# Two thirds of a layer's modulation weights read in another stage, and one third's columns written by themselves

## The chip, the core and the metric

The kernel runs on one core of a Trainium2 chip. A core has a matrix engine (TensorE, PE in the rows; PEld is its weight load), a vector engine (VectorE, DVE), an activation engine (ScalarE, ACT), a general engine (GpSimd, POOL) and SyncE (SP), which here only issues transfers. Each engine works through its own instructions in order and waits on semaphores for the others. Transfers between the chip's memory (HBM) and the core's working memory (SBUF) are issued by SyncE's queue and by GpSimd's queue. Matrix products are summed in PSUM. The metric is the time of one execution in device microseconds (us), lower is better.

## What is computed

The reference is a network of two blocks on 256 tokens of width 1024, all in float32. Cut to what matters here:

```
x  = first_block(x, ...)         # retention + sliding-window attention, gates, w_out;
                                 # then a router and 32 small experts; then a gated extra input
for i in range(2):               # second_block: two layers on x, the first also on ctx
    mod   = (silu(c)     @ w_mod[i] + b_mod[i])        # 6 x 1024 columns
    mod_c = (silu(c_ctx) @ w_mod[i] + b_mod[i])
    sh1, sc1, gt1, sh2, sc2, gt2 = split(mod, 6)
    h  = rms_norm(x, g_norm1[i]) * (1 + sc1) + sh1     # the same for ctx with mod_c
    x  = x + gt1 * mix(h, hc)                          # neighbourhood attention, gating unit,
                                                       # latent attention, gates, w_out
    x  = x + gt2 * squared_relu_mlp(rms_norm(x, g_norm2[i]) * (1 + sc2) + sh2)
```

`w_mod[i]` is 1024 x 6144, 25 MB a layer. Of its six column blocks the first two (shift and scale of the first norm) are wanted when a layer begins, the third behind the mixing, and the last three around the feed-forward part.

## The kernel before

**Weights.** All dense weights come through `piece()` (line 237): SyncE's queue loads 512 KB into a tile `raw` (128 x 1024, line 244), ScalarE copies it into a rounded high part `wh` (line 202), VectorE makes the rest `wl` (line 203), and TensorE does three products for each block of it (lines 260 to 262 and 288 to 290). There are 8 `raw`, 3 `wh` and 3 `wl` tiles (line 73), handed out in the program's order. PSUM tags are `pd` and `cd` (dense products) and `ps` and `cs` (small ones), two buffers each.

**Work beside other work.** `beside(steps, every)` registers a generator, and `advance()`, called by every piece, lets it take one step for each `every` pieces. `drain()` runs what is left of it on the spot.

**Modulation.** `w_mod` (line 770) goes through the six column blocks in three thirds of 2048 columns. A third is 8 steps and a tail. A step takes two `raw` tiles (1 MB, line 779) and makes 8 matmul records with 32-column weights (line 784), straight from `raw`, with no split. The tail takes two more `raw` tiles for the bias rows (line 790) and 8 matmuls (line 795), copies the sum out of PSUM into an activation tile `a2` (`evac`, lines 340 and 342) and writes it to a scratch array `modscr` by four transfers of GpSimd's queue (line 801). Behind the last third two transfers of the same queue bring the whole of `modscr` back as columns, `modcol` (line 803).

**Order.** `run_all` (line 421) is written out by hand. All 24 steps and 3 tails of layer 0 run beside `block1_mix`, one for 1.25 pieces (`MOD_EVERY`, line 74), in PSUM tag `cs`, and are drained. Then come `cl.rows` (norm of ctx; line 1309 makes the scales `modA` of both norms from `modcol`), `block1_out` (line 727, w_out, its sums added to `xres` at line 733), `cl.turn` (lines 396 to 407: ctx is transposed, scaled and shifted), the router (line 805: norm, transposes at line 842, products at line 847, then a long chain of small VectorE work to the slot numbers at line 944), two calls of `fetch` (line 958: eight tiles `ew` with gate weights of the experts, line 962, out of 8 tiles), and `cl.start` (line 1252: 12 pieces of ctx's projections: na_k, na_v, mla_cq). Behind that the experts (line 974; gather of tokens by GpSimd at line 988, transposes at line 1000, gate and up products at line 1010, down products at line 1029) run beside `cl.finish` (line 1254: latent keys, queries and attention, `mla_kv` at line 1477 and 1479 on, na_q, merge, feed-forward). The experts' first step fetches the up weights. Layer 1's modulation runs later, beside the extra input and layer 0 of x, in tag `pd`, and is drained in `x0.finish` just ahead of `kv.rows`, which reads its first two column blocks for ctx.

The activation tiles `a2` of the stage with the router and the experts (stream "c") have three buffers; the router's transposed tokens, the head statistics, mla_cq's output and mla_kv's transposed tokens come from them.

Of the kernel before, what the change touches and what calls it, by code (L numbers as in the profile page):

```python
# [15 lines left out]
ALU = mybir.AluOpType  # L16
# [54 lines left out]


WEIGHTS = (8, 3, 3)
MOD_EVERY = 1.25
AHEAD = 80
LANE = 192
EDGE = 160
# [6 lines left out]
MOD1_EVERY = (1.5, 2.5)  # L84
# [82 lines left out]
class Build:  # L167
# [252 lines left out]
    def run_all(self):  # L420
        nc, tc, i = self.nc, self.tc, self.i
        with ExitStack() as ctx:
            self.P = ctx.enter_context(tc.tile_pool(name="keep", bufs=1))
            self.W = ctx.enter_context(tc.tile_pool(name="weights", bufs=1))
            self.Dr = ctx.enter_context(tc.tile_pool(name="scr", bufs=1, space=DRAM))
            self.psum = ctx.enter_context(tc.tile_pool(name="psum", bufs=1, space=PSUM))
            self.ident = self.P.tile([128, 128], F32, name="ident")
            self.sums = self.P.tile([128, 2, 2, 2], F32, name="sums").rearrange("p s t c -> s p t c")
            self.ints = self.P.tile([128, 16], I32, name="ints")
            self.x = self.P.tile([128, 2, 1024], F32, name="xres")  # L430
            self.mod_input()
            for t in range(2):
                nc.sync.dma_start(self.x[:, t], i["x"][0, t * 128:t * 128 + 128])
            nc.sync.dma_start(self.ident, i["ident"])
            self.modcol = self.P.tile([128, 2, 2, 6, 8], F32, name="modcol")
            self.modscr = [self.Dr.tile([2, 6144], F32, name=f"modscr{l}") for l in range(2)]
            self.kvscr = [self.Dr.tile([128, 5120], F32, name=f"kvscr{l}") for l in range(2)]
            self.ctxscr = self.Dr.tile([128, 2048], F32, name="ctxscr")
            self.X = ctx.enter_context(tc.tile_pool(name="xT", bufs=1))
            ca = ctx.enter_context(ExitStack())  # L440
            self.slots = ca.enter_context(tc.tile_pool(name="slots", bufs=1))
            cl = Layer(self, None, 0, "ctx")
            with ExitStack() as ce:
                early = Stream(self, ce, "e", ACTS_E, ["pd"], ["ps", "cd"])
                mod = self.beside(self.w_mod(early, "cs", 0), MOD_EVERY)
                mh = self.block1_mix(early)
                self.layer_consts(early)
                self.gple = self.gain_col("ple_gate_norm_g")
                self.drain(mod)
                self.loads, self.ready = self.expert_loads(), []  # L450
                cl.rows(early)
                self.block1_out(early, mh)
                cl.turn(early)
            self.dump("x1", self.x)
            cs = Stream(self, ca, "c", ACTS_C, ["cd"], ["cs"])
            cl.st = cs
            with ExitStack() as cr:
                route = Stream(self, cr, "r", {}, ["pd"], ["ps"])
                self.router(route, cs)
                for _ in range(2):  # L460
                    self.fetch()
                cl.start()
            experts = self.beside(self.moe(cs), MOE_EVERY)
            cl.finish()
            self.drain(experts)
            self.dump("x2", self.x)
            self.mst = cs
            mod = self.beside(self.w_mod(None, "pd", 1), MOD1_EVERY[0])
            self.ple(cs)
            ca.close()  # L470
            st = Stream(self, ctx, "b", ACTS_B, ["pd", "cd"], ["ps", "cs"])
            self.mst = st
            mod[1] = MOD1_EVERY[1]
            self.dump("x3", self.x)
            for tag, n in (("ss1", 1), ("nm", 16), ("ny", 16), ("nt", 16)):
                st.small([128, n], tag=tag, bufs=2 if tag == "ss1" else 8)
            st.pool.tile([128, 64], F32, name="gap")
            self.W2 = st.pool
            self.W2.tile([128, 1024], F32R, name="wh", tag="wh", bufs=1)
            st.pad(LANE)  # L480
            kv = Layer(self, st, 1, "kv")
            x0 = Layer(self, st, 0, "x")
            x0.rows(st)
            x0.turn(st)
            x0.start()
            x0.finish(lambda: self.drain(mod), kv)
            self.dump("x4", self.x)
            x1 = Layer(self, st, 1, "x")
            x1.rows(st)
            kv.na_v()  # L490
            x1.turn(st)
            kv.na_k_end()
            chain = self.beside(kv.mla_kv(), KV_EVERY)
            x1.start()
            self.drain(chain)
            x1.finish()
# [270 lines left out]
        self.one = self.P.tile([1, 32], F32, name="one32")  # L767
        nc.vector.memset(self.one, 1.0)

    def w_mod(self, st, tag, l):  # L770
        nc, i = self.nc, self.i
        mm = nc.tensor.matmul
        for j in range(3):
            ps = self.psum.tile([128, 512], F32, name=tag, tag=tag, bufs=2)
            for k in range(8):
                wt = [self.weight(0) for _ in range(2)]
                for u in range(2):
                    c = j * 2048 + u * 1024
# [9 lines left out]
            for u in range(2):  # L788
                c = j * 2048 + u * 1024
# [9 lines left out]
            for g in range(4):  # L799
                c = (4 * j + g) * 512  # L800
                nc.gpsimd.dma_start(self.modscr[l][:, c:c + 512], ev[32 * g:32 * g + 2])
        for r in range(2):
            nc.gpsimd.dma_start(self.modcol[:, l, r], self.modscr[l][r].rearrange("(a p k) -> p a k", a=6, k=8))

    def router(self, st, act):
        nc, i = self.nc, self.i
# [23 lines left out]
        r = self.newton(st, self.sumsq(st, self.x), 2, 1.0 / D)  # L830
        lgT = one.tile([36, 256], F32, name="lgT")
        lps = st.dense()
        xn = act.a(8).rearrange("p (t k q) -> p t k q", t=2, k=8)
        for t in range(2):
            nc.vector.scalar_tensor_tensor(xn[:, t], self.x[:, t].rearrange("p (q k) -> p k q", k=8), r[:, t:t + 1],
# [2 lines left out]
        for j in range(4):  # L838
            ps = st.small_ps().rearrange("p (k t) -> p k t", k=2)
            for kk in range(2):  # L840
                for t in range(2):
                    nc.tensor.transpose(ps[:, kk, t * 128:t * 128 + 128], xn[:, t, 2 * j + kk], self.ident)
            hT = act.a(2).rearrange("p (k t) -> p k t", k=2)
            self.evac(hT, ps)
            for kk in range(2):
                k = 2 * j + kk
                mm(lps[:36, :256], wr[:, k], hT[:, kk], start=k == 0, stop=k == 7)
        nc.vector.tensor_copy(lgT, lps[:36, :256])
        lg = one.tile([128, 2, 36], F32, name="lg")
        ps = st.small_ps()  # L850
        for t in range(2):
            nc.tensor.transpose(ps[:, t * 36:t * 36 + 36], lgT[:, t * 128:t * 128 + 128], self.ident[:36, :36])
        nc.vector.tensor_tensor(lg, ps[:, :72].rearrange("p (t e) -> p t e", t=2),
                                br[:, None, :].to_broadcast([128, 2, 36]), op=ALU.add)
        tl = lambda shape, nm, dt=F32: one.tile(shape, dt, name=nm)
        gl = tl([128, 2, 8], "gl")
        nc.vector.memset(gl, -3.0e38)
# [43 lines left out]
        mm(ps[:, 1], tri[:, 1], M[:, 0], start=False, stop=True)  # L901
        mm(ps[:, 2], tri[:, 1], M[:, 0], start=True, stop=False)
        mm(ps[:, 2], tri[:, 1], M[:, 1], start=False, stop=True)
        rank = tl([128, 3, 32], "rank")
        nc.vector.tensor_copy(rank, ps[:, 0:3])
        cmax = tl([128, 1], "cmax")
# [5 lines left out]
        for t in range(2):  # L912
            for k in range(2):
                nc.vector.tensor_tensor_reduce(out=junk, in0=oh[:, t, k], in1=rank[:, t], scale=1.0, scalar=0.0,
                                               op0=ALU.mult, op1=ALU.add, accum_out=rk[:, t, k:k + 1])
# [26 lines left out]
        for g in range(8):  # L942
            for t in range(2):
                mm(ps[:, g:g + 1], S[:, t, 4 * g:4 * g + 4].rearrange("p e s -> p (e s)"), tok[:, t:t + 1],
                   start=t == 0, stop=t == 1)
        self.sti = self.ints[:, 5:13]
        nc.vector.tensor_copy(self.sti, ps[:, :8])

# [277 lines left out]
class Layer:  # L1226
# [74 lines left out]
    def rows(self, st):  # L1301
        nc, l, b = self.nc, self.l, self.b
        self.load_x(st)
        mc = self.mc = b.modcol[:, l, self.r]
        self.gna, self.gm, self.gmt, self.gqc = (z[:, l] for z in (b.gna, b.gm, b.gmt, b.gqc))
        self.rope = b.rope if self.mode == "x" else None
        A = self.A = b.X.tile([128, 2, 8], F32, name="modA", tag="modA", bufs=3)
        for c in range(2):
            nc.vector.scalar_tensor_tensor(A[:, c], mc[:, 3 * c + 1], 1.0, b.g12[:, l, c], op0=ALU.add, op1=ALU.mult)
        self.xn = b.norm_rows(st, self.x, stats=self.mode == "x")  # L1310

    def turn(self, st):
# [391 lines left out]
    def ffn(self, meanwhile=None):  # L1704
        nc, i, st, b, l = self.nc, self.i, self.st, self.b, self.l
        xn = b.norm_rows(st, self.x, stats=True)
        self.gate_row(5)
        if meanwhile:
            meanwhile()
        xT = b.turn(st, xn, mod=(self.A[:, 1], self.mc[:, 3]))  # L1710
# [52 lines left out]
```

## Time and profile before

| | us |
|---|---|
| three runs, median (lowest to highest) | 1915.82 (1912.88 to 1919.98) |
| the profiled execution | 1904.63 |
| its span, first to last instruction | 1902.9 |
| TensorE busy in the span | 1784.8 (94%) |
| VectorE, ScalarE, GpSimd busy | 1245.9, 917.6, 199.7 |
| mean granted TensorE clock | 0.986 of full speed |
| moved by transfers | 450.57 MB, 237 GB/s in the mean |

The profiled execution is one run; what is read from it is a sum within its own 1904.63 us. Busy time of an engine is the union of its instructions. In the timeline rows the figure in brackets is the idle time of the engine ahead of that instruction, with what ended it; rows of SyncE and GpSimd that issue transfers show the issue and not the transfer.

### The profile page before, as it was taken

The numbers are of one execution on the slowest core, as the hardware profiler recorded it, in microseconds if no ns is written. First come the engines' busy times: TensorE is split into PE (matmuls) and PEld (weight loads), VectorE is DVE, ScalarE is ACT, GpSimd is POOL, SyncE is SP. The second block draws the span as 40 slices with busy tenths as digits, with TensorE's granted clock in tenths as the row PEclk, the third lists the DMA queues.
The fourth block names the chain that finished last, engine by engine and source line by source line (L and its number), as shares of the span: only waits on it lengthen the run. The fifth ranks groups of instructions, "written<-read, shape, count | busy, mean of one in ns | idle before, by whom it ended". The sixth has DMA issues, their size and how long they took to land. (4 is left out here: it accounts for less than half of the span.)

```text
span 1902.9 us, 32459 instructions
## 1 busy us (share of the span) xinstructions
PE 1784.8 (94%) x12572; PEld 1467.1 (77%) x12572; DVE 1245.9 (65%) x2340; ACT 917.6 (48%) x1432; POOL 199.7 (10%) x226
## 2 busy tenths in 40 slices
PE   5998888999999999988999899999999899999998
PEld 3677875777886877764777878799988888788998
DVE  3655875664566545465668596766688787866665
ACT  3533544563344433344535465644456555555443
POOL 4002210100110001110110111011100101000110
PEclk9999998999999999999999999999999999998999
DMA  8788958888999899977787644466667655264662
GB/s 280 259 304 286 337 159 275 288 290 324 333 366 367 314 385 333 353 259 242 255 254 233 190 156 120 146 187 190 198 181 225 183 140 172 79 190 141 191 196 91
DMA packets 277092, 450.57 MB, mean 237 GB/s; under 512 B 35084, under 2 KB 181852, under 8 KB 276488
## 3 DMA queue, kind: packets, MB, share of 16 engines
q1 hardware_dynamic: 266200, 417.27, 66.4%
q0 software_dynamic: 10736, 31.22, 4.9%
q8 instruction: 99, 1.62, 0.3%
q14 instruction: 57, 0.47, 0.1%
HBM read 432.55 MB, written 15.86 MB: 236 GB/s over the span
## 5 line engine op out<-in xcount | busy, mean ns | idle before, releaser
L203 DVE TENSOR_TENSOR wl<-raw,wh 128x1024 fp32r<-128x1024 f32 (+2 forms) x484 | 605.8, 1256 | 317.4 <-ACT wh L202 160.0
L202 ACT ACTIVATE wh<-raw 128x1024 fp32r<-128x1024 f32 (+2 forms) x484 | 504.2, 1045 | 542.7 <-PE pd L261 121.8
L262 PE MATMUL pd<-xT,wl 128*128 128x256 f32 x384 | 109.1, 284 | 5.3 <-DVE wl L203 5.3
L261 PE MATMUL pd<-xT,wh 128*128 128x256 f32 x384 | 108.7, 283 | 0.0
L260 PE MATMUL pd<-xT,wh 128*128 128x256 f32 x384 | 108.4, 282 | 0.1
L262 PE MATMUL pd<-e_a,wl 128*128 128x256 f32 x288 | 82.5, 286 | 6.9 <-DVE wl L203 6.9
L262 PE MATMUL cd<-xT,wl 128*128 128x256 f32 x288 | 82.2, 285 | 3.1 <-DVE wl L203 3.0
L1010 PE MATMUL ps<-ew,m_heT 128*32 128x256 f32 x1024 | 76.5, 387 | 7.3 <-DMA ew<-in_w_exp_up_dram 6.5
L261 PE MATMUL cd<-xT,wh 128*128 128x256 f32 x288 | 82.4, 286 | 0.0
L260 PE MATMUL cd<-xT,wh 128*128 128x256 f32 x288 | 82.0, 285 | 0.0
L260 PE MATMUL pd<-e_a,wh 128*128 128x256 f32 x288 | 81.9, 284 | 0.0
L261 PE MATMUL pd<-e_a,wh 128*128 128x256 f32 x288 | 81.4, 283 | 0.0
L262 PEld LDWEIGHTS pd<-xT,wl 128*128 128x128 f32 x384 | 72.5, 189 | 9.1 <-DVE wl L203 6.0
L261 PE MATMUL cd<-b_a,wh 128*128 128x256 f32 x280 | 77.8, 278 | 0.0
L260 PE MATMUL cd<-b_a,wh 128*128 128x256 f32 x280 | 77.8, 278 | 0.0
L262 PE MATMUL cd<-b_a,wl 128*128 128x256 f32 x280 | 77.5, 277 | 0.0
L288 PE MATMUL cd<-wh,xT 128*128 128x512 f32 (+2 forms) x208 | 73.6, 356 | 1.7 <-ACT xT L202 1.5
L260 PEld LDWEIGHTS pd<-xT,wh 128*128 128x128 f32 x384 | 72.2, 188 | 3.2 <-issue 2.4
L261 PEld LDWEIGHTS pd<-xT,wh 128*128 128x128 f32 x384 | 72.3, 188 | 2.5 <-issue 2.3
L289 PE MATMUL cd<-wl,xT 128*128 128x512 f32 (+2 forms) x208 | 72.6, 349 | 0.1
L290 PE MATMUL cd<-wh,xT 128*128 128x512 f32 (+2 forms) x208 | 72.4, 349 | 0.0
L262 PE MATMUL cd<-c_a,wl 128*128 128x256 f32 x224 | 62.8, 281 | 6.4 <-DVE wl L203 6.4
(775 smaller groups left out, 5034.1 us busy)
## 6 DMA issues: line engine op xcount, KB each, us to landing
raw<-in_ffn_w_dram SPq DMA_DIRECT2D x192, 512.0 KB, 4.7
raw<-in_w_in_dram SPq DMA_DIRECT2D x168, 512.0 KB, 4.7
raw<-in_w_mod_dram SPq DMA_DIRECT2D x96, 512.0 KB, 5.3
ew<-in_w_exp_gate_dram SPq DMA_DIRECT2D x64, 512.0 KB, 7.3
ew<-in_w_exp_up_dram SPq DMA_DIRECT2D x64, 512.0 KB, 8.3
ew<-in_w_exp_down_dram SPq DMA_DIRECT2D x64, 512.0 KB, 6.6
raw<-in_w_out_dram SPq DMA_DIRECT2D x32, 512.0 KB, 6.7
raw<-in_w_in_dram SPq DMA_DIRECT2D x16, 504.0 KB, 4.3
```

What stands on the lines that cost most here:

```text
L202: self.nc.scalar.activation(h, src, AF.Copy)
L203: self.nc.vector.tensor_tensor(l, src, h.bitcast(F32), op=ALU.subtract)
L260: mm(ps, wh[:, s], xh[:, k], start=k == 0, stop=False)
L261: mm(ps, wh[:, s], xl[:, k], start=False, stop=False)
L262: mm(ps, wl[:, s], xh[:, k], start=False, stop=k == n - 1)
L288: mm(ps[t], xh[:, k, s], wh, start=k == 0, stop=False)
L289: mm(ps[t], xh[:, k, s], wl, start=False, stop=False)
L290: mm(ps[t], xl[:, k, s], wh, start=False, stop=k == K - 1)
L1010: mm(pg[32 * e:32 * e + 32, u * 256:u * 256 + 256], heT[:, kh * 4 + k, 32 * e:32 * e + 32], ws[e][:, k], start=kh == 0 and k == 0, stop=kh ...
```

## The change

Layer 0's modulation is split into two generators. The first third runs beside `block1_mix`, one step for 4 pieces. The other two thirds are registered behind block 1 with the sums in PSUM tag `pd`; they take one step at each of five places in the router and, one for 1.6 pieces, seven beside the 12 pieces of `cl.start`; the last four steps and a tail are drained ahead of the experts. The two fetches of expert weights stand ahead of the router. `modcol` is written a third at a time (two transfers for each third), in both layers. `rows` makes only the first norm's scale, and `ffn` (line 1703) makes the second's.

```diff
-MOD_EVERY = 1.25
+MOD0_EVERY = (4.0, 1.6)
...
-                mod = self.beside(self.w_mod(early, "cs", 0), MOD_EVERY)
+                mod = self.beside(self.w_mod(early, "cs", 0, (0,)), MOD0_EVERY[0])
...
             cl.st = cs
+            self.mst = cs
+            for _ in range(2):
+                self.fetch()
+            mod = self.beside(self.w_mod(None, "pd", 0, (1, 2)), MOD0_EVERY[1])
             with ExitStack() as cr:
                 route = Stream(self, cr, "r", {}, ["pd"], ["ps"])
                 self.router(route, cs)
-                for _ in range(2):
-                    self.fetch()
                 cl.start()
+            self.drain(mod)
             experts = self.beside(self.moe(cs), MOE_EVERY)
...
-            mod = self.beside(self.w_mod(None, "pd", 1), MOD1_EVERY[0])
+            mod = self.beside(self.w_mod(None, "pd", 1, (0, 1, 2)), MOD1_EVERY[0])
...
-    def w_mod(self, st, tag, l):
+    def w_mod(self, st, tag, l, thirds):
...
-        for j in range(3):
+        for j in thirds:
...
-        for r in range(2):
-            nc.gpsimd.dma_start(self.modcol[:, l, r], self.modscr[l][r].rearrange("(a p k) -> p a k", a=6, k=8))
+            for r in range(2):
+                nc.gpsimd.dma_start(self.modcol[:, l, r, 2 * j:2 * j + 2],
+                                    self.modscr[l][r, 2048 * j:2048 * j + 2048].rearrange("(a p k) -> p a k", a=2, k=8))
...
         lps = st.dense()
+        self.advance(1.6)
...
                 mm(lps[:36, :256], wr[:, k], hT[:, kk], start=k == 0, stop=k == 7)
+            if j == 3:
+                self.advance(1.6)
...
+        self.advance(1.6)
         tl = lambda shape, nm, dt=F32: one.tile(shape, dt, name=nm)
...
         mm(ps[:, 2], tri[:, 1], M[:, 1], start=False, stop=True)
+        self.advance(1.6)
...
                    start=t == 0, stop=t == 1)
+        self.advance(1.6)
         self.sti = self.ints[:, 5:13]
...
-        for c in range(2):
-            nc.vector.scalar_tensor_tensor(A[:, c], mc[:, 3 * c + 1], 1.0, b.g12[:, l, c], op0=ALU.add, op1=ALU.mult)
+        nc.vector.scalar_tensor_tensor(A[:, 0], mc[:, 1], 1.0, b.g12[:, l, 0], op0=ALU.add, op1=ALU.mult)
...
         self.gate_row(5)
+        nc.vector.scalar_tensor_tensor(self.A[:, 1], self.mc[:, 4], 1.0, b.g12[:, l, 1], op0=ALU.add, op1=ALU.mult)
```

## Rows read from the trace of the kernel before

**Rows 1.** The page: busy time, share of the span and instructions of each engine.

```profile
PE 1784.8 (94%) x12572; PEld 1467.1 (77%) x12572; DVE 1245.9 (65%) x2340; ACT 917.6 (48%) x1432; POOL 199.7 (10%) x226
```

**Rows 2.** Windows by stage: busy us (instructions) of each engine, clock, DMA share and rate.

```profile
core 0: us, PE busy (x) PEld busy (x) DVE busy (x) ACT busy (x) POOL busy (x), PEclk, DMA share, GB/s
60.00:150.00 90.00, 90.00 (x683) 67.11 (x681) 52.66 (x128) 37.45 (x75) 5.04 (x10) 1.00 0.85 291
150.00:182.00 32.00, 26.84 (x204) 22.92 (x201) 15.54 (x15) 8.98 (x10) 6.76 (x12) 0.95 0.91 295
249.70:330.00 80.30, 66.40 (x429) 48.68 (x427) 54.88 (x179) 37.73 (x77) 11.21 (x18) 0.94 0.68 214
330.00:800.00 470.00, 460.71 (x3653) 354.21 (x3656) 265.17 (x418) 204.29 (x313) 46.03 (x43) 1.00 0.93 334
830.00:900.00 70.00, 61.74 (x268) 37.90 (x266) 40.58 (x78) 34.28 (x53) 0.58 (x1) 0.99 0.78 260
40.00:50.00 10.00, 8.46 (x65) 7.30 (x67) 7.45 (x20) 5.43 (x11) 0.00 (x0) 1.00 1.04 404
1070.00:1080.00 10.00, 6.99 (x47) 6.79 (x46) 2.76 (x6) 1.89 (x3) 1.71 (x2) 0.83 0.62 197
```

**Rows 3.** TensorE's timeline: start, duration, line, tile, form, count; one modulation step, one tail.

```profile
29.85 0.39 PE L288 MATMUL pd<-wh,e_a 128*128 128x512 f32 x1
30.08 0.40 PE L289 MATMUL pd<-wl,e_a 128*128 128x512 f32 x1
30.40 1.07 PE L784 MATMUL cs<-raw,sT 128*32 128x512 f32 x8
31.40 0.50 PE L290 MATMUL pd<-wh,e_a 128*128 128x512 f32 x1
...
72.75 1.06 PE L795 MATMUL cs<-raw,one 1*32 1x512 f32 x8
```

**Rows 4.** Instructions of line 784 in PSUM tag cs: min/median/max ns, first and last start.

```profile
L784 PE MATMUL cs<-raw,sT x192: 592/617/1059, 24.4 to 160.5; 128*32 128x512 f32 x192
```

**Rows 5.** SyncE's queue at the start: start, time until the next issue, line, tile, count.

```profile
12.12 10.96 SPq L779 DMA_DIRECT2D raw<-in_w_mod_dram  x2
26.32 0.38 SPq L244 DMA_DIRECT2D raw<-in_w_in_dram  x1
```

**Rows 6.** TensorE's timeline, two waits of the stretch 150 to 182 with what released them.

```profile
164.17 0.39 PE L262 MATMUL pd<-e_a,wl 128*128 128x256 f32 x1 [1.61 <-DVE wl L203]
...
177.04 0.38 PE L262 MATMUL pd<-e_a,wl 128*128 128x256 f32 x1 [2.41 <-DVE wl L203]
```

**Rows 7.** ScalarE's timeline: the evacuation of layer 0's last third.

```profile
167.93 0.60 ACT L340 ACTIVATE e_a<-cs 128x512 f32<-128x512 f32 x1 [7.19 <-PE cs L795]
```

**Rows 8.** SyncE's queue, 215 to 325 us.

```profile
234.20 24.18 SPq L244 DMA_DIRECT2D raw<-in_w_in_dram  x9
...
281.71 24.52 SPq L244 DMA_DIRECT2D raw<-in_w_in_dram  x8
307.92 6.07 SPq L962 DMA_DIRECT2D ew<-in_w_exp_up_dram  x8
```

**Rows 9.** VectorE's timeline: the last accumulation of block 1's output.

```profile
247.97 1.28 DVE L733 TENSOR_TENSOR xres<-pd,xres 128x512 f32<-128x512 f32 x2
```

**Rows 10.** TensorE's timeline, 297 to 320 us.

```profile
300.97 0.47 PE L288 MATMUL cd<-wh,c_a 128*128 128x512 f32 x1
...
315.19 1.06 PE L1010 MATMUL ps<-ew,m_heT 128*32 128x256 f32 x2 [5.18 <-DMA ew<-in_w_exp_up_dram]
```

**Rows 11.** GpSimd, VectorE and TensorE around 1070 us, behind layer 1's last third.

```profile
1070.40 1.71 POOL L803 DMA_DIRECT2D modcol<-modscr  x2 [6.29 <-DMA modscr<-b_a]
...
1074.40 0.17 DVE L1309 SCALAR_TENSOR_TENSOR modA<-modcol,g 128x8 f32<-128x8 f32 x1 [6.93 <-DMA modcol<-modscr]
...
1075.86 0.39 PE L262 MATMUL cd<-xT,wl 128*128 128x256 f32 x1 [3.01 <-DVE wl L203]
```

**Rows 12.** SyncE's waits between 330 and 830 us: us, times, longest.

```profile
SPq L962 <- PE ps L1010: 142.5, 29, 12.8
```

## The prediction

> **What bounds the kernel now.** The page's first line comes first: TensorE is busy for 1784.8 of 1902.9 us of span [rows 1], so all its idle time together is 118 us. The change moves TensorE's work and removes none; it can gain only what it takes from that idle time, or from stretches at a lower clock. The windows by stage tell where that lies [rows 2]. From 60 to 150 us, where layer 0's modulation runs beside block 1, TensorE has no idle time at all: each modulation step there pushes everything behind it. From 150 to 182 it is idle for 32 − 26.84 = 5.2 us, at a clock of 0.95. From 249.7, the end of block 1, to 330, the stage of the router and of ctx's first projections, it is idle for 80.3 − 66.40 = 13.9 us, and transfers run at a share of 0.68, 214 GB/s. From 330 to 800 the waits add up to 470 − 460.71 = 9.3 us in 470, and SyncE's queue itself waits there for TensorE to free the expert tiles, 142.5 us in 29 waits [rows 12]: that stage is TensorE's, and what reaches it late is late at the end. So the sum has three places: the time saved ahead of 249.7, the time lost from there to 330, and the round trip at 1070.
>
> **Block 1: 18 items leave.** Two thirds are 16 steps and 2 tails. What one costs is read between the neighbours of a step in TensorE's timeline: the product ahead of it starts at 30.08 and the one behind it at 31.40, where consecutive products of that width start 0.23 apart (29.85 and 30.08), so a step takes 31.40 − 30.08 − 0.23 = 1.09 us; a tail shows the same 1.06 [rows 3]. 18 × 1.09 = 19.6 us. All 192 records of the layer lie between 24.4 and 160.5 [rows 4], most of it in the stretch with no idle time. Not all of it is gained: from 40 to 50 us TensorE is idle for 1.5 us [rows 2], in a gap of the attention, and a step that lies in such a gap costs nothing. Two of the 18 I take to lie so: −2.2.
>
> Two waits go with them. At the start SyncE sits 10.96 us on the modulation's third pair, since the eight tiles are full, and block 1's fourth tile of weights is issued only at 26.32 [rows 5]. With one step for 4 pieces the first four tiles go out together. I take 2 us, from 0 (the first product is set by the split) to 4. From 150 to 182 TensorE waits for split weights, twice for 1.61 and 2.41 us, while ScalarE, which makes them, stands 7.19 us in front of the evacuation of layer 0's last third [rows 6, 7]. That evacuation leaves. What would be late next is VectorE's part of the position bias, which fills the same stretch and stays. Idle 5.2 and clock (1 − 0.95) × 32 = 1.6 make 6.8 us; I take half, 3.5. **Ahead of 249.7: −19.6 + 2.2 − 2 − 3.5 = −22.9**, between −17 and −27.
>
> **Router and ctx's projections: 18 items arrive.** By TensorE's work the stage needs 66.4 + 19.6 = 86.0 us and has 80.3: if every idle microsecond were filled, it would take +5.7. Two idle times are new. The modulation's sums move to the tag that block 1's output holds until its last accumulation at 247.97 to 249.3 [rows 9], and in the program's order the pairs of the first steps stand ahead of ctx's weights: the first four pairs fill the eight tiles and can't be used until that moment. Now nine loads of ctx's weights are issued by 258 [rows 8] and some are split by then. So the first ctx product waits for a tile to come free, a transfer and a split; in place of a row for that I take the 5.18 us that TensorE waits for the up weights [rows 10], from 0 to 8. And part of the 13.9 us is no room that modulation can fill, since the engine's order is fixed and a step behind a waiting product waits with it. I take that as 3 us. 5.7 + 5 + 3 = 13.7.
>
> By the transfers, independently: the stage moves 80.3 × 214 = 17.2 MB, and 16 steps add 16 × 2 tiles of 0.524 MB, 16.8 MB, to 34.0. At the 334 GB/s of 330 to 800 that takes 101.8 us (+21.5), at the 404 of 40 to 50 it takes 84.2 (+3.9) [rows 2]; midway, at 369, 92.1 (+11.8). The up weights stand behind it all on SyncE's queue, issued at 307.92 behind eight tiles of na_q [rows 8]. **From 249.7 to 330: +14**, the larger of the two, between +6 and +22. The page "DMA: Bandwidth & Descriptors" of the Trainium skill (section Specifications) gives some 358 GB/s as the limit of a core's traffic with HBM; the 404 measured here in 10 us is above it, so the measurement decides; by the page 34.0 MB would take 95 us, an estimate, +14.7 in place of +11.8.
>
> The latent keys' first product is at 300.97 now [rows 10]; it falls behind the drained steps and behind the last evacuation, which takes one of three a2 buffers. Its own cost is within the +14 if other products stand ahead of it, else it is rival C. On GpSimd's queue, each third adds a round trip: the column transfers wait for the scratch transfers, 6.29 us, and issue for 1.71 [rows 11]; behind them stand the gather of the experts' tokens and the key scratch. Up to 8 us there, hidden while TensorE has modulation to do; I take 0. In layer 1 the same wait stands ahead of GpSimd's share of the head norms; 0, up to 6. The fetches of gate weights wait for nothing that the router makes, and the eight tiles are free, so moving them is worth 0. The second norm's scale is one VectorE instruction of 0.17 us [rows 11], moved to the feed-forward part: 0 behind its norm, 0.2 a layer if uncovered.
>
> **Layer 1's round trip.** kv.rows reads two column blocks, but the columns are written only behind the last third: GpSimd waits 6.29 us, VectorE 6.93, and TensorE stands for 3.01 us until 1075.86 [rows 11]; from 1070 to 1080 the clock averages 0.83 [rows 2], which loses another 0.17 × 10 = 1.7. By thirds, its columns are there since the first third. **−4.7**; 0 if the columns are awaited as a whole.
>
> **Sum.** −22.9 + 14 − 4.7 = −13.6. Against the profiled 1904.63 that is 1891; this one run lies 11.2 below the median of the three timed, 1915.82, so I put the difference on the median: **1902**. Counted as idle time it closes: 3.0 at 1070, 2 at the start, 2.6 before 182 and 13.9 − (80.3 + 14 − 86.0) = 5.6 in the router's stage, less the 2.2 of the gaps that stay empty, make 11.0; the clock gives 1.7 and 0.9.
>
> **The rivals.** A, the forecast: 1902, by itself 1895 to 1910. B, the idle time of the router stage is filled wholly: for it speaks that transfers have room there (0.68) and that modulation needs no split; against, the full ring at its start. −22.9 + 5.7 − 4.7 = −21.9: 1894. C, about no change: the stream of weights goes at the 334 GB/s of the expert stage and no faster, the up weights come late and the chain of the latent attention with them; +21.5 gives −6.1: 1910, and with the columns awaited as a whole (−1.4) 1914. For it speaks that 404 is seen in 10 us only. "Perfetto Trace Analysis" of the Trainium skill (Identifying the Most-Contended Engine) has one improve the engine with the most work; TensorE's work stays the same, so by it alone nothing is gained. The stretches with 5.2 and 13.9 us of idle time say that there is more to be had than work. D, slower: eight tiles are too few for two streams. From 830 to 900, where layer 1's modulation runs beside few pieces, transfers come to 260 GB/s only and TensorE is idle for 8.3 us of 70 [rows 2]. A step's pair stays in the ring until its matmuls, in order behind a waiting router, free it. At 260, 34.0 MB take 131 us, +50, at the 291 of block 1 117, +36.5: with −27.6 that is +9 to +23, midway +16: 1932. It decides when the stage costs more than 27.6, below 34.0 MB / 107.9 us = 315 GB/s, and beyond +37, below 290, it shows. Against it: in both of those stretches TensorE, or a chain, sets the pace, and here TensorE needs only 86 us for the bytes.
>
> **How the numbers follow.** A 0.42, B 0.20, C 0.22, D 0.16. About 0.5%, 9.6 us, is what a measurement of this kernel can tell from no change: 1906.2 to 1925.4. Faster: B and seven tenths of A, 0.50. Within: the rest of A, C, and a little of D, 0.35. Slower: most of D, 0.15. The range, 1887 to 1922, takes B with −27 ahead of 249.7 at its low end and C with the open costs of GpSimd's queue at its high end; out are most of D and a little at the ends of B and C.
>
> **What would show it.** Line 784 should stand with 64 records in tag cs ahead of 160 us and 128 in pd behind block 1. Right for the first step: w_out's last sum near 226 in place of 249, and no wait of ScalarE for line 795 at 168. For the stage: its length from that sum to the first up products some 14 longer, transfers near 370 GB/s, TensorE's idle time about 8; wrong if the first ctx product comes over 8 us behind the sum, if the rate stays below 315, or if the up weights are waited for by much over 5. For the round trip: no wait at line 1309 ahead of kv's first product. The prediction is wrong at its root if TensorE's waits from 330 to 800 rise above 9.3 by more than a few us, since then the chain and not the work came late.

## The result, and the profile after

| | us | ratio to before, 95% interval |
|---|---|---|
| before, in the same timing | 1915.68 (1912.88 to 1919.98) | |
| after | 1935.51 (1932.41 to 1937.40) | 1.0112 (1.0087 to 1.0136) |
| after, a second timing | 1932.64, before 1914.08 | 1.0108 (1.0085 to 1.0130) |

The change makes the kernel about 20 us slower; the forecast was 1902, and 1887 to 1922. Executions of one and the same kernel differ by up to 24 us here (before: 1904.12 to 1928.05 in the runs below), so single parts are weighed by ratios of many runs, and their us are a difference of ratios times 1915. For after that is 1.0110, the mean of the two timings, or 21 us.

The traced execution of before that the prediction read was one of its shortest, 1904.63. A second trace of the same kernel (`before_again`, below) took 1915.89, and its span of 1914.1 lies 19.7 below the 1933.8 of after, as the medians do. Lines of before in this part are from that second trace.

The page's line of busy time, after:

```profile
PE 1805.5 (93%) x12572; PEld 1478.9 (76%) x12572; DVE 1242.3 (64%) x2339; ACT 916.9 (47%) x1432; POOL 211.2 (11%) x234
```

TensorE does the same 12572 instructions as in [rows 1], in 1805.5 us of busy time; the two traces of before have 1784.8 and 1794.8. Where the time lies is told by windows (columns as in [rows 2]) from the start to block 1's last sum, and from there to the first product of ctx's latent attention with the values, a mark that both kernels pass in the same order. First the second trace of before:

```profile
0.00:249.80 249.80, 217.86 (x1512) 172.33 (x1513) 146.06 (x291) 101.57 (x157) 46.73 (x81) 0.99 0.85 288
249.80:353.30 103.50, 88.69 (x549) 66.05 (x547) 70.29 (x212) 50.26 (x99) 14.98 (x23) 0.92 0.68 214
```

and after:

```profile
0.00:230.70 230.70, 204.25 (x1401) 169.23 (x1402) 142.60 (x288) 99.13 (x155) 44.67 (x73) 0.99 0.76 241
230.70:373.90 143.20, 115.56 (x684) 70.54 (x681) 75.97 (x224) 51.82 (x100) 22.02 (x35) 0.90 0.80 279
```

Block 1 ends 19.1 us earlier, the stage of the router takes 39.7 more, and behind it nothing moves: the experts' last down product starts at 824.2 where it started at 804.7 (+19.5), and the end is at +19.7. In the stage TensorE's idle time rose from 103.5 − 88.69 = 14.8 to 143.2 − 115.56 = 27.6 us, where the forecast let it fall to about 8, and its busy time by 26.9. Most of that is the modulation, 14 of whose 18 moved items run here (four ran ahead of block 1's end):

```profile
L787 PE MATMUL pd<-raw,sT 128*32 128x512 f32 x96 | 19.6, 658 | 2.1 <-DMA raw<-in_w_mod_dram 2.1
L798 PE MATMUL pd<-raw,one 1*32 1x512 f32 x16 | 3.2, 600 | 0.0
```

That is 22.8 us, where 14 items at the forecast's 1.09 are 15.3. Another 3.0 us are products of the experts (line 1039) that stood behind the mark before. TensorE's waits there, after (us in all, times, longest):

```profile
PE cs L1526 <- DVE c_a L1571: 7.6, 1, 7.6
PE ps L1010 <- DMA m_he<-xnscr,ints: 5.7, 1, 5.7
PE cd L290 <- DVE c_a L203: 5.6, 1, 5.6
```

Before, that list was led by 6.4 us for up weights (the wait of [rows 10]) and 3.5 for the gather; the first and the third of after stood nowhere. The first and the third have their reason on VectorE's timeline, after:

```profile
324.88 0.43 DVE L203 TENSOR_TENSOR c_a<-c_lr,c_a 128x256 fp32r<-128x256 f32 x1 [4.67 <-DMA modscr<-c_a]
...
331.23 0.17 DVE L1717 SCALAR_TENSOR_TENSOR modA<-modcol,g 128x8 f32<-128x8 f32 x1 [3.77 <-DMA modcol<-modscr]
...
1104.07 0.17 DVE L1717 SCALAR_TENSOR_TENSOR modA<-modcol,g 128x8 f32<-128x8 f32 x1 [6.45 <-DMA modcol<-modscr]
```

At 324.88 VectorE wants an a2 tile for the latent keys' low part, and the tile still holds the last third's sums until they are written to the scratch array. At 331.23 it stands in front of line 1717, the second norm's scale. That line belongs to the feed-forward part of ctx, which comes hundreds of us later; its inputs are there once the last columns land, and the planner (the step that puts the program's instructions into the order in which each engine runs them) put it right there, in front of work that was due. The same line at 1104.07 is layer 1's: it replaces the wait of line 1309 in [rows 11], 6.93 then, 6.45 now.

### The profile page after: what moved, and what is told of

Its sections match the earlier page's. It is cut to its first block, busy times and chain, and to the rows that moved or that the text cites. A ratio compares the mean times of both kernels' runs of the same rounds, so it can differ in the third digit from the quotient of the medians.

```text
span 1933.8 us, 32466 instructions
## 1 busy us (share of the span) xinstructions
PE 1805.5 (93%) x12572; PEld 1478.9 (76%) x12572; DVE 1242.3 (64%) x2339; ACT 916.9 (47%) x1432; POOL 211.2 (11%) x234
## 5 line engine op out<-in xcount | busy, mean ns | idle before, releaser
L1691 POOL TENSOR_TENSOR xres<-xres,b_a 128x512 f32<-128x512 f32 x24 | 37.5, 1562 | 307.6 <-DVE b_a L1689 307.6
```

What stands on the lines that cost most here:

```text
L1691: (nc.vector if stats else nc.gpsimd).tensor_tensor(xs, xs, tmp, op=ALU.add)
```

## The experiments

The rival theories were four: the moved work itself in a fixed order (W); transfers and the ring of eight `raw` tiles, the prediction's rival D (R); the waits behind the last third, for its tile and for its columns (L); and the smaller parts of the change, the fetches and the split of the columns (S).

**The kernel before, again, and the split of the columns alone.** `before_again` is the kernel before, unchanged.

> The kernel before, unchanged, for a second trace: the two traces differ by 30.9 us where the timed medians differ by 19.8. If the 11 us are a matter of the single execution that was traced, this trace lies at 1913 to 1920, and its waits and its clock show where the first one was shorter. If the trace itself comes out near 1904.6 again, the time of a traced execution differs from that of a timed one.

Measured 1915.89, span 1914.1: the first trace was a short execution, and no one place makes it so; it leads by 0.5 us at block 1's end, 4.2 at the experts' last product and 11 at the end.

`thirds_block1` has all 24 steps beside block 1, the columns by thirds and the second norm's scale in the feed-forward part (the edit in `rows`, which then makes only the first scale, isn't shown):

```diff
-        for r in range(2):
-            nc.gpsimd.dma_start(self.modcol[:, l, r], self.modscr[l][r].rearrange("(a p k) -> p a k", a=6, k=8))
+            for r in range(2):
+                nc.gpsimd.dma_start(self.modcol[:, l, r, 2 * j:2 * j + 2], ...)
...
+        nc.vector.scalar_tensor_tensor(self.A[:, 1], self.mc[:, 4], 1.0, b.g12[:, l, 1], op0=ALU.add, op1=ALU.mult)
```

> The kernel before with one part of the change alone: columns written by thirds, and the second norm's scale made in the feed-forward part on VectorE; all 24 steps stay beside block 1 at one in 1.25 pieces. The prediction's step (the wait ahead of kv's first product goes, 3.0 us and 1.7 of clock): 4.7 faster, 1911. Rival: the scale of layer 1's second norm is issued on VectorE right behind the last columns' transfers, as the trace of after shows at 1104.07 with 6.45 us of wait, so the same wait comes back under another line: within 1 us of before, 1915 to 1917.

Measured 1917.09, ratio 1.0008 (0.9980 to 1.0035): no gain. Its trace has the wait under its new line, in VectorE's waits between 1040 and 1120 us,

```profile
DVE modA L1708 <- DMA modcol<-modscr: 6.8, 1, 6.8
```

and TensorE's behind it, in its timeline:

```profile
1088.10 0.39 PE L262 MATMUL cd<-xT,wl 128*128 128x256 f32 x1 [2.85 <-DVE wl L203]
```

`thirds_block1_gpsimd` makes the scale on GpSimd, as (s·g) + g:

```diff
-        nc.vector.scalar_tensor_tensor(self.A[:, 1], self.mc[:, 4], 1.0, b.g12[:, l, 1], op0=ALU.add, op1=ALU.mult)
+        nc.gpsimd.tensor_tensor(self.A[:, 1], self.mc[:, 4], b.g12[:, l, 1], op=ALU.mult)
+        nc.gpsimd.tensor_tensor(self.A[:, 1], self.A[:, 1], b.g12[:, l, 1], op=ALU.add)
```

> The same with the second norm's scale made by GpSimd (two instructions) in place of VectorE. If the wait of VectorE for the last columns is what gave the gain back, it now stands on GpSimd, TensorE no longer waits ahead of kv's first product, and the time is 4 to 5 below that of the same kernel with VectorE: 1911. If the scale has nothing to do with it: no difference.

Measured 1913.58, ratio 0.9999 (0.9979 to 1.0018), 3.5 below the one with VectorE by their medians; the intervals overlap, so the size is not settled. The trace shows the mechanism: the wait now stands on GpSimd, and TensorE has none ahead of kv's first product.

```profile
1080.69 0.45 POOL L1708 TENSOR_TENSOR modA<-modcol,g 128x8 f32<-128x8 f32 x1 [3.24 <-DMA modcol<-modscr]
```

**The waits behind the last third.** `scale_gpsimd` is the changed kernel with those two lines on GpSimd.

> The changed kernel with the second norm's scale made by GpSimd. Theory: VectorE's waits of 3.77 us at 331 and 6.45 us at 1104 stand in the way of ctx's latent keys and of kv's weights; without them TensorE's waits of 7.56 and 2.52 us shrink by about 3.8 and 2.5, and some slow clock with them: 5 to 9 us less than after, 1927 to 1931. Rival: ctx's stage is late by the work and the transfers, and what VectorE waits for is hidden behind them: 1933 to 1936.

Measured 1927.93, ratio 1.0073 (1.0044 to 1.0102), some 7 us of the 21. TensorE's wait of 7.56 us is now 4.75, the one of 2.52 at 1105 is gone. `own_tile` copies the sums of the moved thirds into another tile:

```diff
-            ev = (st or self.mst).a(2)
+            ev = st.a(2) if st else self.mst.a(2, tag="tg" if l == 0 else "a2")
```

> The changed kernel with the sums of layer 0's second and third thirds copied into a tile of the gates' tag, idle at that time, in place of one of the three a2 tiles. TensorE's wait of 5.62 us at 325, ahead of the latent keys' third product, has VectorE waiting for the transfers to the scratch array to free that tile. If the waits add up: 5 to 6 us less than after, 1930. If they stand behind one another (VectorE still waits until 331 for the last columns, for the second norm's scale): 0 to 2 less, 1934 to 1936.

Measured 1927.79, ratio 1.0057 (1.0032 to 1.0083), some 10 us of the 21 by the ratios (7.7 and 4.9 below the two timings of after by the medians, where 5 to 6 were expected): the waits add up rather than stand behind one another. Not wholly: the wait of 5.62 is gone, and the next one, with VectorE's wait for the columns in it, grew from 7.56 to 9.13:

```profile
336.91 0.66 PE L1526 MATMUL cs<-ident,c_a 128*96 128x128 f32 x2 [9.13 <-DVE c_a L1571]
```

`both` has the two edits together.

> The changed kernel with the tile of the gates' tag and with the second norm's scale on GpSimd. Theory that the two waits stand behind one another and both must go: 12 to 14 us less than after, 1922, and ctx's latent keys some 9 us earlier than in after. Rival: the sum of the work and of the transfers sets the stage, the up weights or the gather take over: no more than with GpSimd's scale alone, 1928.

Measured 1921.83, ratio 1.0032 (1.0007 to 1.0058), where 1922 was expected. By the windows of the same stage, `both`:

```profile
233.30:353.90 120.60, 106.64 (x657) 66.27 (x655) 72.86 (x213) 52.06 (x100) 22.90 (x39) 0.96 0.89 307
```

the stage is 120.6 us long, with 14.0 of idle time, as much as before the change: 17.1 longer than before's 103.5 (the trace is of a short execution, 1909.20, its clock 0.96 where before's was 0.92). Theory L holds for these two: together they are worth 1.0110 − 1.0032, about 15 us.

**The items, their work and their transfers.** `left_out` leaves out the 16 steps and the two bias products of layer 0's second and third thirds; their columns are zero.

```diff
         for j in thirds:
+            if l == 0 and j > 0:
+                ev = self.mst.a(2)
+                nc.vector.memset(ev, 0.0)
+                self.mod_out(l, j, ev)
+                continue
...
```

(`mod_out` holds the six transfers that stood at the end of each third.)

> The changed kernel without the 16 steps and the 2 bias products of layer 0's second and third thirds (their columns are zero; the round trip through the scratch array stays): what block 1 gives back, alone, and by the difference to after what the 18 items cost in the router's stage. By the two traces: block 1 ends 19 us earlier, so 19 below before, 1894 to 1898, and the 18 items cost 38 to 42 us where 19.6 us of work is in them. Rival: some ten of these 40 us come from the split of the columns, the scale and the order, not from the items: 1903 to 1908.

Measured 1891.06, ratio 0.9864 (0.9831 to 0.9898), a little below the 1894 to 1898 expected. Block 1 ends at 227.3, 22.5 before, and the stage is as long as before, with 12.1 us of idle time:

```profile
227.30:328.30 101.00, 88.87 (x549) 66.04 (x547) 69.55 (x215) 48.60 (x97) 21.98 (x35) 0.90 0.71 221
```

So the step "block 1 gives back 22.9" was right, and the 18 items cost 1935.5 − 1891.1 = 44 us in and behind the router's stage for 19.6 us of work; these 44 include the waits of theory L. `no_transfers` keeps the products and drops the transfers; the products read the residual tile, so the columns are not the modulation's.

```diff
-                wt = [self.weight(0) for _ in range(2)]
-                for u in range(2):
+                held = l == 0 and j > 0
+                wt = [self.x[:, u] for u in range(2)] if held else [self.weight(0) for _ in range(2)]
+                for u in () if held else range(2):
```

> The changed kernel with the 16 steps' products made from the residual tile that lies in SBUF in place of weights: the products, their order and the round trips stay, 16.8 MB of transfers and 32 uses of the ring of eight tiles go. If the transfers and the ring set the stage (the prediction's slower rival): most of the 40 us goes, 1900 to 1908. If TensorE's work in its fixed order and the waits behind the last third set it: the 7 us of waiting for transfers at the stage's start go, and little else, 1926 to 1930.

Measured 1924.29, ratio 1.0053 (1.0036 to 1.0070): without 16.8 MB of transfers and with 198 GB/s in the stage, the kernel is still slower than before. Transfers and the ring are about 11 us of the 44; R as the main cause falls. The 11 overlap with the 15 of theory L: in this trace the waits behind the last third are 0.9 and 4.4 us, where after has 5.6 and 7.6, and the stage's idle time is 14.6. No run drops the transfers with both waits mended, so what they still cost there isn't shown.

`half` is `both` with two thirds beside block 1 and one beside the router:

```diff
-MOD0_EVERY = (4.0, 1.6)
+MOD0_EVERY = (2.0, 1.6)
...
-                mod = self.beside(self.w_mod(early, "cs", 0, (0,)), MOD0_EVERY[0])
+                mod = self.beside(self.w_mod(early, "cs", 0, (0, 1)), MOD0_EVERY[0])
...
-            mod = self.beside(self.w_mod(None, "pd", 0, (1, 2)), MOD0_EVERY[1])
+            mod = self.beside(self.w_mod(None, "pd", 0, (2,)), MOD0_EVERY[1])
```

> As the kernel with both waits mended (own tile, scale on GpSimd), but with thirds one and two beside block 1, one step for 2 pieces, and only the last third (8 steps and a tail, 9.8 us of work) beside the router. If every item costs its 1.09 us in the router's stage as in block 1, moving is worth nothing: half the loss of that kernel or less, 1914 to 1919. If the stage's 14 us of idle time can be filled by the first few items: 9.8 saved, 3 or less paid, 1906 to 1910.

Measured 1919.88, ratio 1.0018 (0.9997 to 1.0039), just above what W expects, and far from the 1906 to 1910 of filled gaps. The stage again has as much idle time as before, 15.0 us:

```profile
250.40:362.60 112.20, 97.23 (x590) 65.42 (x588) 72.01 (x212) 51.45 (x100) 21.39 (x33) 0.95 0.80 267
```

But in this trace block 1 gives hardly anything back either: it ends at 250.4, with four steps of the last third (3.64 us) ahead of its end and a clock of 0.93 over the first 50 us, where the second trace of before had 1.00. So `half` says that the stage's gaps were not filled; it doesn't say by itself that the move pays as much as it takes. `late` is `both` without the five steps in the router:

```diff
-MOD0_EVERY = (4.0, 1.6)
+MOD0_EVERY = (4.0, 0.75)
...
-        self.advance(1.6)
```

> As the kernel with both waits mended, but no step in the router: all 16 beside ctx's 12 pieces, one for 0.75 pieces. The pairs then stand behind the first piece in the ring. If the ring's first pairs, loaded beside w_out, hold up block 1's end (230.7 where it is 227 without them) and the first ctx product, 4 to 8 us less than with the five steps in the router: 1914 to 1918. If only the work counts: the same, 1920 to 1923. If the last third then ends behind the latent keys: more than that, 1926 and up.

Measured 1921.80, ratio 1.0023 (1.0003 to 1.0042), the same as `both`. Block 1 ends at 226.5, 6.8 ahead of `both`, and the router's first transposes come 12.8 us behind its last sum, in place of 18.9 in `both`; but the stage is 133.2 us long, 12.6 more than there, with 21.2 of idle time: what is gained at its start is lost later. For the time, where the steps lie in the stage didn't matter.

**The fetches.** `fetch_back` is the changed kernel with the two fetches behind the router again.

```diff
-            for _ in range(2):
-                self.fetch()
...
                 self.router(route, cs)
+                for _ in range(2):
+                    self.fetch()
                 cl.start()
```

> The changed kernel with the two fetches of gate weights behind the router again. The prediction has this part at nothing: the transfers wait for no one. 1933 to 1937, as after. Rival: ahead of the router the eight tiles, 4.2 MB, take transfer time from w_out and from the modulation's first pairs; then behind the router it is 3 or more less.

Measured 1930.17, ratio 1.0066 (1.0045 to 1.0087). Since after had been timed at another time, three more kernels ran together: after itself, `both` with the fetches back, and before with nothing but the fetches ahead of the router (the same edit, made the other way).

> The changed kernel, unchanged, beside the kernels it is compared with: the single parts are so far set against 1935.5, which was timed at another time. If the kernel with the fetches back (1930.2) differs from it by its fetches, this lies at 1934 to 1937 here too; if the 5 us are a difference between the timings, it lies at 1929 to 1932.

> Own tile, scale on GpSimd and the fetches behind the router again: the three side effects of the change taken back, its move of two thirds kept. If the fetches cost 5 us ahead of the router: 1916 to 1918, level with before. If they cost nothing: 1920 to 1923, as with the two.

> The kernel before with the two fetches ahead of the router and nothing else of the change. By the prediction nothing: 1913 to 1917. If moving them ahead takes transfer time from ctx's first weights in every case: 1918 to 1921.

After 1.0108 (1.0085 to 1.0130), so the difference to `fetch_back` is no matter of the timing, though the two intervals just touch; `both_fetch_back` 1913.02, 1.0002 (0.9987 to 1.0018), a step of 0.3% from `both`, whose interval overlaps with it; `fetch_early` 1915.55, 1.0014 (0.9994 to 1.0034), nothing that can be told from zero. So by two pairs, which point the same way and are each just at the edge of the noise, the fetches cost 6 to 8 us beside the moved thirds; without them no cost shows.

The trace of `both_fetch_back` is as long as its median (1912.52) and has before's clock in the stage, so it shows the move by itself:

```profile
0.00:229.70 229.70, 204.58 (x1400) 170.29 (x1400) 142.76 (x288) 98.99 (x155) 44.87 (x73) 0.98 0.76 243
229.70:353.20 123.50, 107.65 (x659) 67.69 (x657) 73.45 (x214) 52.01 (x100) 22.94 (x39) 0.92 0.86 300
```

Block 1 ends 20.1 us earlier than in the second trace of before, the stage is 20.0 longer, and its idle time is 15.8 for 14.8.

The fetches' cost is not one of their transfers: SyncE issues the eight tiles at nearly the same time with the fetches ahead of the router (first row, after) and behind it (second row, `fetch_back`), since the planner takes both far forward (the rows are the first four of the eight):

```profile
106.52 2.10 SPq L972 DMA_DIRECT2D ew<-in_w_exp_gate_dram  x4
```

```profile
107.38 1.86 SPq L972 DMA_DIRECT2D ew<-in_w_exp_gate_dram  x4
```

What differs is TensorE's order in the router. In after a step of line 787 is cut into three by the router's transposes:

```profile
259.67 1.05 PE L787 MATMUL pd<-raw,sT 128*32 128x512 f32 x2
260.65 0.33 PE L847 MATMUL ps<-ident,c_a 128*128 128x128 f32 x1
260.90 1.05 PE L787 MATMUL pd<-raw,sT 128*32 128x512 f32 x2
261.88 0.33 PE L847 MATMUL ps<-ident,c_a 128*128 128x128 f32 x1
262.14 1.05 PE L787 MATMUL pd<-raw,sT 128*32 128x512 f32 x4
```

and takes 3 × 1.05 for the 1.07 of [rows 3]. After has three of its steps and tails cut between 231 and 268 (233.15 to 238.2, these, and a tail in two); `fetch_back` has a whole step at 232 and a whole tail at 264 and cuts only the step at 258 (and, later, one in two at 275). At about 1 us for each further piece that is 5 us of cuts for 3, an estimate: 2 of the 6 to 8. The router's slot numbers start at 274.2 there and at 280.3 in after, and the gather's wait is 2.06 us for 5.66. But `both`, with the fetches ahead and the same three cuts, has its slot numbers at 280.1 and a gather's wait of 1.85 only, so that wait doesn't follow from the fetches' place alone. How the fetches come to cost the rest stays open; no run changed the cuts by themselves.

## Why the prediction was wrong, point by point

**Block 1, −22.9.** Right: 22.5 by `left_out`. In after the last sum stands at 230.7 and not at 227, because four steps ran as one group ahead of block 1's last two products. The prediction held that they could not run before block 1's last sum, and its sum had their work in the next stage:

```profile
225.64 3.64 PE L787 MATMUL pd<-raw,sT 128*32 128x512 f32 x32
229.21 0.51 PE L289 MATMUL pd<-wl,e_a 128*128 128x512 f32 x1
```

**The router's stage, +14.** This is the term that failed: it was +39.7, or 43 with those four steps, and outside its bounds of 6 to 22. The sum had the work at 19.6 and let idle time fall by 5.6. The work came in full and more: the 14 items that ran in the stage took 22.8 us in after and 19.3 in `both_fetch_back` (lines 787 and 798), for 15.3 by the price of block 1, with steps cut by other products and part of the time at a lower clock. And with every side effect mended no idle time was filled in sum: 15.8 in `both_fetch_back`, 14.0 in `both`, 15.0 in `half`, 21.2 in `late`, 14.8 before. The waits are not the same ones: that for the up weights fell from 6.4 to 2.6 in `both_fetch_back`, while others stand in front of the router's transposes (2.8), the modulation's own transfers (3.0) and the latent keys (2.6). The prediction named the reason, an order that is fixed when the kernel is built ("a step behind a waiting product waits with it"), and gave it 3 us; that it is this order that makes new waits for those that were filled is argued from these rows and not shown by a run of its own. "Perfetto Trace Analysis" of the Trainium skill (Identifying the Most-Contended Engine), which rival C cited, has one optimize the most-contended engine first. The move left TensorE's work as it was, and with its side effects taken back it is worth nothing (1.0002), which agrees.

**Waits priced at nothing.** The sum had the a2 tile "within the +14", GpSimd's round trip at "I take 0", and the second norm's scale at "0 behind its norm". Here lie most of the other 20 us. The two figures of the round trip held (6.29 and 1.71 in [rows 11], 5.29 and 1.50 here); what it hides behind was wrong. From the last third's last product (316.97) to the first use of its columns (331.23) it is 14 us, and the drained third is the last thing ahead of ctx's latent keys, so its tile and its columns are awaited where TensorE's order has little else. Tile and scale together are about 15 us by the runs. The waits that show are 5.6, 4.2 of the 7.6 (3.4 are left in `both`) and the 2.5 in layer 1; behind the first two the clock is low, which costs about 1.7 us each time, an estimate from these two rows:

```profile
325.30:329.30 4.00, 3.94 (x9) 2.18 (x10) 0.85 (x3) 1.76 (x4) 1.50 (x2) 0.57 1.04 418
339.10:345.00 5.90, 5.54 (x24) 2.82 (x24) 1.75 (x5) 2.58 (x4) 0.00 (x0) 0.72 0.77 284
```

A clock of 0.57 or 0.72 is a mixture of the two levels, 1.2 and 2.4 GHz: most of the first stretch and rather more than half of the second at the lower one. The same is seen behind the gather's wait of 5.66, where the clock is 0.50 from 298.8 to 304.8 with TensorE busy throughout.

**The start of the stage, 5 us in place of a row.** The first ctx product starts at 239.44, 8.7 us behind the sum, where it was 2.1 in the second trace of before: 6.6 more, within 0 to 8, so the term was about right; by the prediction's own sign ("over 8 us behind the sum") the step was wrong by 0.7. The other sign that it gave for a chain, waits behind the stage, moved little: over the same work, 330.3 to 800.3 in the second trace of before and 350 to 820 in after, TensorE's idle time is 9.1 and 12.0.

**Layer 1's round trip, −4.7.** Nothing was gained: TensorE waits 2.52 us there in after, 2.76 in the second trace of before. The step took the wait to belong to the columns of kv's first norm. It belongs to whatever reads the last third's columns first on VectorE, and the change made a new reader, free to be planned at that place. With the scale on GpSimd the wait of TensorE is gone (`scale_gpsimd`, `thirds_block1_gpsimd`). Even then no gain can be told from zero, and the full 4.7 lie just outside the interval of `thirds_block1_gpsimd` (0.9979 at its low end, some 4 us).

**The fetches, 0.** The reason given (the transfers wait for nothing) holds by SyncE's rows; the price doesn't, 6 to 8 us beside the moved thirds, by a way that is only partly seen.

**Rival D, 1932 with a chance of 0.16,** hit the time and not the cause. It put the loss on the stream of weights. The rate did stay below its bound of 315 (279 GB/s), yet with no transfers of the moved steps 1.0053 remains, about half of the loss, and with the transfers kept and the side effects mended it is gone.

**The ledger,** in ratios: after 1.0110; the scale and the tile mended, 1.0032; the fetches back, 1.0002. What is left is the move itself: it takes some 20 us out of one stage, where the work costs TensorE's full time, and pays as much in another. No kernel that does all the work is clearly faster than the one before.

## What to carry to other kernels

Idle time of an in-order engine is room only for work that its fixed order puts into that very gap: before moving work into a stage for its idle share, name for each gap which instruction would stand in it, and else count the work in full. A load that is drained last in a stage can show its round trip, so count its tile, its copy and each first reader of its result, on every engine. An instruction moved to a later part of the source isn't moved on its engine unless something holds it there; look where its inputs become ready.

## What the runs showed of the hardware

Four column groups of 32 run side by side on TensorE only while their instructions stand together. One record lasts 0.59 us, yet a whole step of 8 records takes 1.07 us [rows 3] and a run of four steps 3.64 us for 32 records (0.91 a step). A group of 2 records alone, between two transposes, takes 1.05, and by the starts 0.98 (259.67 to 260.65). Cutting a step in three nearly triples its price.

The same kernel's executions differ by up to 24 us (1904.12 to 1928.05), and two traces of it by 11.2 (mean clock 0.986 and 0.981 of full speed). A difference of traces of that size needs a second trace of the kernel before.
